# A two-layer streaming encoder on one core: plain first pairs and combinations made behind them

## Chip, cores and metric

The kernel runs on one core of a Trainium2 chip. The metric is the time of one execution in microseconds (us); lower is better. PE is TensorE, DVE is VectorE, ACT is ScalarE, POOL is GpSimd, SP is SyncE, whose queue issues the weight loads.

## What is computed

Two layers work on 656 tokens (16 meta and 512 prompt tokens, 8 x 16 sample tokens) of width 1024:

```
def swiglu(x, w_gate, w_up, w_down):
    return (jax.nn.silu(x @ w_gate) * (x @ w_up)) @ w_down
h = x + 0.5 * swiglu(rmsnorm(x, n1), f1g, f1u, f1d)
u = rmsnorm(h, nm)
...                         # pooling, gated convolution and attention on u @ w_in, gated and summed
h = h + mixed @ w_out
out = h + 0.5 * swiglu(rmsnorm(h, n2), f2g, f2u, f2d)
```

The feed-forward width is 2816, that is 22 column blocks of 128. The change is in the four feed-forward stages (two in each layer); the mixer between them stays.

## The kernel before, in words

Activations lie transposed: H holds 8 row blocks (m) of 128 features by 656 tokens. Every fp32 operand is split into a high and a low fp32r part, and a product is three matmuls (`mm3`, line 140). A split (`split`, line 145) is a copy on ACT and a subtraction on DVE (line 129).

**Strassen pairs.** Two weight columns make a pair. Four row blocks against four others, and the first half of the tokens against the second, give x as four blocks B11, B12, B21, B22 for each row pair (k, k+4). `combine` (line 529) multiplies them by the norm's gain and the old scale, makes four differences (Q1, T3, Q2, T4) and splits the seven that are used into XR, 2296 columns at once. `run_pair` (line 628) then makes seven products instead of eight, each of 4 k x 3 = 12 matmuls of 128x328 (`seven`, line 674), into three PSUM banks: the bank "mm" takes products 1, 4, 6 and 7 one on top of the other and is copied out by ACT after the first three of them, two banks "z" take the others. The seventh is put behind the first product of the unit that follows (`late`). A stage has 11 pairs, each a gate unit and an up unit; in the last stage the halves have 320 columns.

**Weights.** SP loads 512 KB blocks into four raw buffers; each unit splits seven slabs of 128x512 from them into a ring of nine slots (`ffn_columns`, line 250; one of them lies in XR). Four sums of weights for each unit are made on POOL (`sums`, line 386, recorded as line 389).

**Entry of a stage.** While the last 8 down or w_out units finish the row blocks of H in the order 0, 4, 1, 5, 2, 6, 3, 7, `feed` (line 503) squares each on ACT, adds the squares on POOL (line 518) and calls `combine` for a row pair when its second block is done. At the end the sum is split, `scales` (line 557) multiplies it by a matrix of 1/1024 in two fp32r matmuls, and the factor is made for the evictions. In the first stage `begin` (line 1137) transposes the tokens, makes the scale of both halves and then combines the four row pairs.

**Order.** What one engine does is in order. The order of each engine's instructions is fixed when the program is built: a scheduler runs the program against estimated durations and takes the ready instruction that stands first in the program. `pump` (line 357) is where the program asks for loads and slab splits.

Of the kernel before, what the change touches and what calls it, by code (L numbers as in the profile page):

```python
# [5 lines left out]
F32 = mybir.dt.float32  # L6
F32R = mybir.dt.float32r
# [39 lines left out]
XC = 2 * 4 * 7 * 328  # L47
# [4 lines left out]
WARM = 9  # L52


class Builder:
    def __init__(self, nc, tc, pools, t):
        self.nc, self.tc, self.t = nc, tc, t
        self.sb, self.wp, self.rp, self.pp = pools
        self.halves = HALF_ALL
        self.jobs = []  # L60
        self.job = self.before = None
        self.mid, self.end = [], []
        self.clock = 1
        self.held = [False, False]
        self.taken = False
        self.bank_i = 0
        self.uid = 0
# [5 lines left out]
        self.fed = 0  # L73


        self.spots = {"slab": [None] * 4, "raw": [None] * 2}
        self.spot_i = {"slab": 0, "raw": 0}
        self.busy = {"slab": [], "raw": []}
# [72 lines left out]
    def setup(self):  # L151
# [6 lines left out]
        self.ones = sb.tile([P, P], F32R, tag="ones", name="ones")  # L158
# [13 lines left out]
        self.sqs = [self.XR[:, XC + 656 * i:XC + 656 * (i + 1)] for i in range(2)]  # L172
# [27 lines left out]
        self.copies = [W[:, o + 1312 * i:o + 1312 * (i + 1)] for i in range(2)]  # L200
        self.parts = W[:, o:o + 2624]
        self.sq_row = W[:, o:o + DM]
        self.ms = W[:, o + 1024:o + 1030]
        self.rows = [W[:, o + 2000:o + 2128], W[:, o + 2128:o + 2256]]
# [4 lines left out]
        self.na_f, self.nb_f = W[:, o + 1968:o + 2296], W[:, o + 2296:o + 2624]  # L209
        o += 2624  # L210
        self.s3 = [W[:, o + 512 * i:o + 512 * (i + 1)] for i in range(2)]
        o += 1024
        assert o <= WA
# [289 lines left out]
    def feed(self, to, l, m, hi):  # L503

        c0, c1 = self.halves[hi]
        gain = {"mixer": "mix_norm", "ffn1": "ffn1_norm", "ffn2": "ffn2_norm"}[to]
        if to == "mixer":
            self.gained(self.H[:, m, c0:c1], l, m, c0, c1, gain)
        if hi == 0:
            return  # L510
        c0 = self.halves[0][0]
        n = c1 - c0
        acc, s = self.acc[:, :n], self.sq[self.fed % 2][:, :n]
        if self.fed == 0:
            self.act(acc, self.H[:, m, c0:c1], AF.Square)
        else:
            self.act(s, self.H[:, m, c0:c1], AF.Square)
            self.nc.gpsimd.tensor_tensor(acc, acc, s, op=ALU.add)  # L518
        self.fed += 1
        if to != "mixer" and m >= 4:  # L520
            self.combine(l, m - 4, gain)
# [7 lines left out]
    def combine(self, l, j, gain):  # L529


        c0, c1 = self.halves[0][0], self.halves[1][1]
        n = (c1 - c0) // 2
        p = self.parts[:, :8 * n].rearrange("p (q c) -> p q c", q=8)
        two = lambda a: a.rearrange("p (t c) -> p t c", t=2)
        scale = two(self.rstd[:, c0:c1])
        for m, out in ((j, p[:, 0:8:7, :]), (j + 4, p[:, 1:3, :])):
            self.stt(out, two(self.H[:, m, c0:c1]), self.col(gain, l, m), scale, ALU.mult, ALU.mult)
        b11, b21, b22, q1, t3, q2, t4, b12 = (p[:, i, :] for i in range(8))
        self.sub(p[:, 3:5, :], p[:, 0:3:2, :], b12.unsqueeze(1).broadcast_to([P, 2, n]))  # L540
        self.stt(q2, q1, -1.0, b22, ALU.mult, ALU.subtract)
        self.stt(t4, q2, -1.0, b21, ALU.mult, ALU.subtract)
        hi, lo = (self.XR[:, self.xc(s, j, 0, n):self.xc(s, j, 7, n)] for s in range(2))
        self.split(hi, lo, self.parts[:, :7 * n])

    @staticmethod
    def xc(s, k, q, n):
        return (s * 4 + k) * 7 * 328 + q * n
# [56 lines left out]

    def ffn_ready(self):
        self.ffn_raw()
        self.Ra = self.sb.tile([P, 2, 6, T], F32R, tag="Ra", name=self.name("ra"))

    def ffn_units(self, l, which, to):  # L610
        t = self.t
        g, up, dn = (t[f"ffn{which}_w_{s}"] for s in ("gate", "up", "down"))
        units, down = [], []
        for ci, (f0, fn) in enumerate(CHUNKS):
            for i in range(fn):
                f = 2 * (f0 + i)
                units.append(self.pair_unit(g[l], f, self.gate_out))
# [4 lines left out]
            for m in (0, 4, 1, 5, 2, 6, 3, 7):  # L622
                down.append(self.unit(k, [(0, k, dn[l][r0:r0 + k * P, m * P:(m + 1) * P])], self.hu_down, "F",
                                      m=m, l=l, scale=0.5, to=to if ci == len(CHUNKS) - 1 else None,
                                      last=ci == len(CHUNKS) - 1))
        return units + down

    def run_pair(self, u):
# [4 lines left out]
        p1, u2, u3, p5 = (self.copies[u["turn"]][:, i * n:(i + 1) * n] for i in range(4))  # L633
# [5 lines left out]
        self.seven(u, b1, 0, n, True)  # L639
        self.act(p1, b1[:, :n], AF.Copy)  # L640
# [4 lines left out]
        self.seven(u, b3, 1, n, True)  # L645
        self.tt(s[0], b3[:, :n], p1, ALU.add)
        self.pump(1)
        self.seven(u, b2, 3, n, True)
        self.act(p5, b2[:, :n], AF.Copy)
        self.pump(1)  # L650
        self.seven(u, b1, 5, n, False)
        self.act(u2, b1[:, :n], AF.Copy)
        self.pump(1)
        self.seven(u, b2, 2, n, False)
        self.tt(s[1], b2[:, :n], u2, ALU.add)
# [3 lines left out]
        self.seven(u, b1, 4, n, False)  # L659
        self.act(u3, b1[:, :n], AF.Copy)  # L660
        self.tt(s[3], u3, p5, ALU.add)
# [3 lines left out]
        def last():  # L665
            self.late = None
            self.seven(u, b1, 6, n, False)
# [6 lines left out]
    def seven(self, u, bank, q, n, start):  # L674
# [3 lines left out]
        for k in range(4):  # L678
            x = [self.XR[:, self.xc(s, k, q, n):self.xc(s, k, q + 1, n)] for s in range(2)]
# [395 lines left out]
    def mixer_units(self, l):  # L1075
# [32 lines left out]
        for m in (0, 4, 1, 5, 2, 6, 3, 7):  # L1108
# [28 lines left out]
    def begin(self):  # L1137

        nc, xt = self.nc, self.xt
        nc.vector.memset(self.factor, 1.0)  # L1140
        for hi in range(2):
            c0, c1 = HALF_ALL[hi]
            n = c1 - c0
            sums = self.psum("aux")
            for i, o, rows in self.TOKENS[hi]:
                ms = self.ms[:rows, i:i + 1]
                self.act(self.sq_row[:rows, :], xt[:rows, i, :], AF.Square, scale=DM ** -0.5, accum_out=ms)
            for m in range(KD):
                ps = self.psum(("z", "z", "z", "z", "mm", "mm", "z", "z")[m])
                for i, o, rows in self.TOKENS[hi]:  # L1150
                    nc.tensor.transpose(ps[:, o:o + rows], xt[:rows, i, m * P:(m + 1) * P],
                                        self.ident[:rows, :rows])
                nc.vector.tensor_copy(self.H[:, m, c0:c1], ps[:, :n])
            for i, o, rows in self.TOKENS[hi]:
                self.mm(sums[:, o:o + rows], self.ms[:rows, i:i + 1].broadcast_to([rows, P]), self.ident[:rows, :rows],
                        o == 0, False)
            self.scale_of(sums[:, :n], c0, c1, False, self.sil, self.up)
        for j in range(4):
            self.combine(0, j, "ffn1_norm")
            self.pump()  # L1160
        self.Ra = self.sb.tile([P, 2, 6, T], F32R, tag="Ra", name=self.name("ra"))
# [328 lines left out]
```

## Time and profile before

| | |
|---|---|
| median of 3 runs | 2926.77 us (2923.93 to 2928.16) |
| profiled execution, its time / its span | 2924.71 us / 2923.0 us |
| PE, DVE, ACT, POOL busy | 97%, 69%, 45%, 22% of the span |
| granted TensorE clock, mean | 0.982 of full speed |
| PE matmuls | 19083 |

Busy shares are averages over stages with different limits. Matmuls are pipelined, so a busy PE is not PE at its peak; the number of matmuls in a stretch of known length says more. A clock of 1.00 is the 2.4 GHz level, 0.5 the 1.2 GHz level. Lines are often those of a helper (129 is any two-input DVE operation, 126 any with a scalar, 115 any activation, 138 any matmul), so tiles tell the operations apart: XR holds the blocks and combinations of x, "ws" and "slabs" are weight slabs, "mm", "z" and "aux" are PSUM banks, "Wa" is scratch space.

### The profile page before, as it was taken

Reading aid. Unit: us, or ns where it says so; the run is one execution under the profiler, and the core shown is the slowest. Engines: PE = TensorE matmul, PEld = TensorE weight load, DVE = VectorE, ACT = ScalarE, POOL = GpSimd, SP = SyncE. Lnnn points to the kernel's source line nnn. Section 1 sums busy time; section 2 is a strip of 40 time slices with the busy share of each in tenths; the row PEclk is TensorE's granted clock in tenths of the full one; section 3 lists DMA queues with packets and bytes.
Section 4 is the critical chain, followed back from the end, with each engine's and each line's share of the span. In section 5 each row is a group of like instructions: output and inputs, shape, how many; then the busy total and the mean of one; then the engine's idle time right before and its main releaser. Section 6 shows DMA issues by size and latency. Waiting matters only on the chain.

```text
span 2923.0 us, 47652 instructions
## 1 busy us (share of the span) xinstructions
PE 2831.0 (97%) x19083; PEld 2781.1 (95%) x19083; DVE 2003.9 (69%) x3234; ACT 1322.4 (45%) x2545; POOL 652.8 (22%) x518
## 2 busy tenths in 40 slices
PE   4999999999999989999989999999999998999999
PEld 3999999999999989999979999998999998999999
DVE  7775766776444787675887866758764457975864
ACT  3443534667422354443444534446763333543533
POOL 2332232011000152232243232310110003432230
PEclk6999999999999999999989999999999999999999
DMA  2322322222222223322212222222222222322322
GB/s 83 92 64 84 87 77 70 80 73 75 62 77 73 73 69 91 87 69 84 80 48 83 83 77 87 73 75 71 76 75 66 73 76 83 87 69 83 87 76 69
DMA packets 437169, 224.26 MB, mean 77 GB/s; under 512 B 10111, under 2 KB 436291, under 8 KB 436947
## 3 DMA queue, kind: packets, MB, share of 16 engines
q1 hardware_dynamic: 436452, 220.90, 26.0%
q8 instruction: 149, 2.44, 0.3%
q14 instruction: 74, 0.60, 0.1%
q10 hardware_dynamic: 494, 0.32, 0.0%
HBM read 212.87 MB, written 8.31 MB: 76 GB/s over the span
## 4 chain that ended last, share of the span: by engine, by line
PE 85%; DVE 10%; issue 2%; ACT 2%; DMA 1%; POOL 1%; SPq 0%; ACTq 0%; DVEq 0%; POOLq 0%
PE z L138 50%; PE mm L138 33%; DVE Wa L129 2%; DVE Wa L126 2%; DVE slabs L129 2%; DVE ws L129 2%; DVE XR L129 1%; ACT XR L115 1%; PE aux L138 1%; DVE ra L129 1%; DVE H L126 0%; DMA rawb<-in_ffn_w_up_dram 0%; POOL raw L389 0%; POOL Wa L389 0%; DMA raw<-in_ffn_w_gate_dram 0%
## 5 line engine op out<-in xcount | busy, mean ns | idle before, releaser
L138 PE MATMUL mm<-XR,ws 128*128 128x328 f32 (+3 forms) x4788 | 800.7, 316 | 43.4 <-ACT XR L115 30.5
L138 PEld LDWEIGHTS mm<-XR,ws 128*128 128x128 f32 x4788 | 734.5, 189 | 53.4 <-ACT XR L115 32.0
L138 PE MATMUL z<-XR,ws 128*128 128x328 f32 (+3 forms) x3480 | 559.0, 314 | 7.1 <-DVE ws L129 7.1
L138 PEld LDWEIGHTS z<-XR,ws 128*128 128x128 f32 x3480 | 532.0, 190 | 8.6 <-DVE ws L129 8.5
L129 DVE TENSOR_TENSOR ws<-raw,ws 128x512 fp32r<-128x512 f32 (+1 forms) x413 | 312.3, 759 | 167.2 <-ACT ws L115 166.0
L115 ACT ACTIVATE ws<-raw 128x512 fp32r<-128x512 f32 (+1 forms) x413 | 253.7, 616 | 315.0 <-PE z L138 177.0
L138 PE MATMUL z<-ra,ws 128*128 128x328 f32 (+1 forms) x2520 | 395.6, 312 | 0.0
L138 PEld LDWEIGHTS z<-ra,ws 128*128 128x128 f32 x2520 | 379.9, 188 | 0.4 <-DVE H L126 0.3
L138 PE MATMUL mm<-XR,slabs 128*128 128x328 f32 (+1 forms) x1932 | 323.2, 314 | 11.3 <-ACT XR L115 5.5
L138 PEld LDWEIGHTS mm<-XR,slabs 128*128 128x128 f32 x1932 | 298.0, 189 | 15.1 <-DVE Wa L126 6.6
L138 PE MATMUL z<-ra,slabs 128*128 128x328 f32 (+1 forms) x1836 | 288.3, 312 | 0.4 <-DVE ra L129 0.4
L138 PEld LDWEIGHTS z<-ra,slabs 128*128 128x128 f32 x1836 | 277.6, 188 | 1.1 <-DVE ra L129 1.0
L129 DVE TENSOR_TENSOR Wa<-Wa 128x656 f32<-128x656 f32 (+5 forms) x328 | 253.3, 782 | 18.3 <-ACT Wa L115 14.2
L126 DVE SCALAR_TENSOR_TENSOR H<-z,H 128x328 f32<-128x328 f32 (+1 forms) x288 | 140.8, 492 | 140.3 <-PE z L138 139.9
L138 PE MATMUL z<-XR,slabs 128*128 128x328 f32 (+1 forms) x1356 | 224.9, 314 | 4.0 <-DVE H L126 2.9
L138 PEld LDWEIGHTS z<-XR,slabs 128*128 128x128 f32 x1356 | 209.3, 190 | 4.9 <-DVE H L126 3.5
L518 POOL TENSOR_TENSOR Wa<-Wa 128x656 f32<-128x656 f32 (+1 forms) x35 | 64.9, 1854 | 630.7 <-ACT Wa L115 626.8
L115 ACT ACTIVATE Wa<-Wa 128x656 f32<-128x656 f32 (+8 forms) x232 | 137.4, 598 | 120.3 <-DVE Wa L129 99.0
L129 DVE TENSOR_TENSOR slabs<-rawb,slabs 128x512 fp32r<-128x512 f32 (+1 forms) x167 | 143.6, 861 | 46.3 <-ACT slabs L115 34.3
L115 ACT ACTIVATE slabs<-raw 128x512 fp32r<-128x512 f32 (+1 forms) x163 | 98.2, 604 | 163.3 <-PE z L138 84.5
L115 ACT ACTIVATE slabs<-rawb 128x512 fp32r<-128x512 f32 (+1 forms) x167 | 100.2, 601 | 152.1 <-PE z L138 81.2
L389 POOL TENSOR_TENSOR rawb<-rawb 128x512 f32<-128x512 f32 x97 | 144.1, 1488 | 101.2 <-DVE ws L129 53.8
(179 smaller groups left out, 3508.2 us busy)
## 6 DMA issues: line engine op xcount, KB each, us to landing
raw<-in_w_in_dram SPq DMA_DIRECT2D x88, 512.0 KB, 3.7
raw<-in_ffn_w_gate_dram SPq DMA_DIRECT2D x57, 512.0 KB, 3.6
rawb<-in_ffn_w_up_dram SPq DMA_DIRECT2D x55, 512.0 KB, 3.6
rawb<-in_ffn_w_down_dram SPq DMA_DIRECT2D x48, 384.0 KB, 3.5
raw<-in_ffn_w_down_dram SPq DMA_DIRECT2D x48, 384.0 KB, 3.5
raw<-in_ffn_w_up_dram SPq DMA_DIRECT2D x33, 512.0 KB, 3.6
rawb<-in_ffn_w_gate_dram SPq DMA_DIRECT2D x31, 512.0 KB, 3.7
raw<-in_w_out_dram SPq DMA_DIRECT2D x16, 512.0 KB, 4.0
```

Of the source, the lines that this page charges most:

```text
L115: i = self.nc.scalar.activation(out, in_, func, **kw).ins
L126: return self.nc.vector.scalar_tensor_tensor(out, in0, scalar, in1, op0=op0, op1=op1).ins
L129: self.nc.vector.tensor_tensor(out, in0, in1, op=op)
L138: self.nc.tensor.matmul(out, lhsT, rhs, start=start, stop=stop, skip_group_check=True)
L389: add = lambda out, a, b: self.nc.gpsimd.tensor_tensor(out, a, b, op=ALU.add)
L518: self.nc.gpsimd.tensor_tensor(acc, acc, s, op=ALU.add)
```

## The change

- The first pair of each stage is plain: four units of one column (`col_unit`), 2 slabs each, 8 k x 3 matmuls for each token half, no weight sums; the rest stay Strassen pairs.
- x lies in XR as four blocks and four combinations. Blocks are split when their row of H arrives; combinations of the first two row pairs are made during the last units of the stage before, those of the other two behind the plain products (`todo`).
- In the first stage the first token half is prepared and split before the second, and the four plain columns take the first half, then the second (`by_half`).
- The sum of squares is not split any more: `ones` is fp32 and one fp32 matmul takes the sum. The last square is added on DVE.
- In a Strassen unit the third product of the bank "mm" is no longer copied by ACT; DVE adds from the bank.
- The slab ring in a feed-forward stage has eight slots, because XR is full.

```diff
-        at = [W[:, i * SLAB:(i + 1) * SLAB] for i in range(4)] + [self.XR[:, XC + 1312:XC + 1312 + SLAB]]
+        at = [W[:, i * SLAB:(i + 1) * SLAB] for i in range(4)]
...
+        if to != "mixer":
+            self.blocks(l, m, gain, c0, n // 2)
...
+            if self.fed == KD - 1:
+                self.tt(acc, acc, s, ALU.add)
+            else:
+                self.nc.gpsimd.tensor_tensor(acc, acc, s, op=ALU.add)
...
-            sq = [a[:, :n] for a in self.sqs]
-            self.split(sq[0], sq[1], acc)
...
+    def blocks(self, l, m, gain, c0, n):
+        j, r = m % 4, m // 4
+        p = self.part(j)[:, 2 * n * r:2 * n * (r + 1)]
+        self.stt(p, self.H[:, m, c0:c0 + 2 * n], self.col(gain, l, m), self.rstd[:, c0:c0 + 2 * n], ALU.mult, ALU.mult)
+        self.split(*(self.xs(s, j, 2 * r, n, 2) for s in range(2)), p)
+        if r:
+            self.todo.append(lambda: self.combine(j, n))
+            if j in (1, 2):
+                self.todo.pop(0)()
+    def combine(self, j, n):
+        p = self.part(j)[:, :4 * n]
+        self.mix(*(p[:, i * n:(i + 1) * n] for i in range(4)))
+        self.split(*(self.xs(s, j, Q2, n, 4) for s in range(2)), p)
+    def mix(self, b11, b12, b21, b22):
+        self.sub(b22, b22, b12)
+        self.sub(b12, b11, b12)
+        self.stt(b11, b11, -1.0, b22, ALU.mult, ALU.subtract)
+        self.stt(b21, b11, -1.0, b21, ALU.mult, ALU.subtract)
...
-            for i in (1, 0):
-                self.mm(ps, self.ones, self.sqs[i][:, c0 - at:c1 - at], i == 1, i == 0)
+            self.mm(ps, self.ones, self.acc[:, c0 - at:c1 - at], True, True)
...
+    def run_col(self, u):
+        slabs = self.use(u, 2)
+        u["w"] = [(ws, k) for ws, _ in slabs for k in range(4)]
+        cols = [(u, 0), (u, 1)]
+        if self.by_half:
+            self.held_cols.append((u, slabs))
+            cols = [(u, 0)]
+            if "last_col" in u:
+                cols += [(v, 1) for v, _ in self.held_cols]
+        for v, hi in cols:
+            self.slot_start()
+            self.half_col(v, hi)
+            if self.by_half and hi:
+                self.used(self.held_cols.pop(0)[1])
+            if self.todo and not (self.by_half and hi == 0 and v is self.held_cols[0][0]):
+                self.todo.pop(0)()
+            self.pump()
+            self.slot_tail()
...
+    def half_col(self, u, hi):
+        (c0, c1), r = self.halves[hi], u["r"]
+        n = c1 - c0
+        x = lambda s, k, a, b: self.xs(s, k % 4, 2 * (k // 4) + hi, n)
+        ps = self.product(self.psum("z"), u["w"], x, SLOTS, SLOTS, c0, c1)
+        S = self.sil if u["evict"] == self.gate_out else self.up
+        self.mul(S[:, (2 * r + hi) * n:(2 * r + hi + 1) * n], ps, self.factor[:, c0:c1])
+        if hi:
+            u["evict"](u, r, n)
...
-        self.act(u3, b1[:, :n], AF.Copy)
-        self.tt(s[3], u3, p5, ALU.add)
+        self.tt(s[3], b1[:, :n], p5, ALU.add)
...
+        sums = [self.tokens(0)]
+        self.token_scale(0, sums[0])
+        self.pump(2)
+        first = [self.parts[:, 328 * m:328 * (m + 1)] for m in range(KD)]
+        self.first_blocks(0, first)
+        sums.append(self.tokens(1))
+        self.token_scale(1, sums[1])
+        self.pump(2)
+        more = self.sb.tile([P, KD * 328], F32, tag="Ra", name="xpart")
+        second = [more[:, 328 * m:328 * (m + 1)] for m in range(KD)]
+        self.first_blocks(1, second)
+        for j in range(4):
+            self.todo.append(lambda j=j: self.first_combine(j, first, second))
```

## Rows read from the trace of the kernel before

**Rows 1.** The page: PE's busy time, the granted clock in 40 slices, the last chain.
```profile
PE 2831.0 (97%) x19083; PEld 2781.1 (95%) x19083; DVE 2003.9 (69%) x3234; ACT 1322.4 (45%) x2545; POOL 652.8 (22%) x518
...
PEclk6999999999999999999989999999999999999999
...
PE 85%; DVE 10%; issue 2%; ACT 2%; DMA 1%; POOL 1%; SPq 0%; ACTq 0%; DVEq 0%; POOLq 0%
```

**Rows 2.** Stretches: length, PE, PEld, DVE, ACT, POOL busy (instructions), clock, DMA, GB/s.
```profile
41.00:75.00 34.00, 20.59 (x73) 17.96 (x74) 24.50 (x25) 9.54 (x10) 0.00 (x0) 0.61 0.02 5
75.00:100.00 25.00, 25.00 (x168) 25.00 (x167) 19.77 (x28) 13.23 (x25) 10.44 (x7) 1.00 0.30 89
100.00:150.00 50.00, 49.98 (x333) 49.71 (x332) 37.68 (x57) 20.98 (x39) 13.86 (x10) 1.00 0.31 90
1031.00:1055.00 24.00, 16.03 (x79) 15.09 (x78) 22.91 (x22) 9.61 (x17) 18.18 (x10) 0.72 0.30 88
1055.00:1100.00 45.00, 43.72 (x288) 43.10 (x288) 40.69 (x62) 26.19 (x50) 16.50 (x10) 1.00 0.24 71
1484.00:1520.00 36.00, 22.04 (x92) 19.31 (x91) 32.15 (x40) 16.68 (x25) 13.92 (x7) 0.67 0.10 29
2471.00:2495.00 24.00, 14.89 (x88) 14.10 (x87) 22.96 (x23) 11.13 (x19) 17.50 (x10) 0.86 0.30 88
2495.00:2530.00 35.00, 32.17 (x217) 31.39 (x216) 33.90 (x48) 19.07 (x36) 14.94 (x9) 1.00 0.26 76
```

**Rows 3.** Waits of PE, whole run: us in total, times, longest.
```profile
PE mm L138 <- ACT XR L115: 36.1, 5, 21.9
PE aux L138 <- DVE XR L129: 11.8, 3, 6.2
PE mm L138 <- DVE Wa L126: 8.5, 13, 1.5
```

**Rows 4.** Timeline of DVE at the second stage's entry: start us, us, instruction.
```profile
1036.97 0.48 DVE L126 SCALAR_TENSOR_TENSOR H<-z,H 128x328 f32<-128x328 f32 x1
1037.38 0.68 DVE L129 TENSOR_TENSOR slabs<-raw,slabs 128x512 fp32r<-128x512 f32 x1
...
1038.85 2.00 DVE L129 TENSOR_TENSOR slabs<-raw,slabs 128x512 fp32r<-128x512 f32 x1
...
1047.50 2.57 DVE L129 TENSOR_TENSOR XR<-Wa,XR 128x2296 fp32r<-128x2296 f32 x1 [0.98 <-ACT XR L115]
```

**Rows 5.** The start: DVE's slab splits from 15 to 30 us; timeline to 50 us.
```profile
15.00:30.00 15.00, 10.29 (x8) 0.66 0.25 69
...
29.72 0.54 DVE L126 SCALAR_TENSOR_TENSOR scale<-Wa 128x384 f32<-128x384 f32 x1
...
40.98 0.64 PE L138 MATMUL mm<-XR,ws 128*128 128x328 f32 x1 [21.93 <-ACT XR L115]
...
43.55 1.84 DVE L126 SCALAR_TENSOR_TENSOR Wa<-H,cols,scale 128x656 f32<-128x656 f32 x2
...
45.42 0.84 DVE L129 TENSOR_TENSOR Wa<-Wa 128x656 f32<-128x656 f32 x1
...
49.52 2.55 DVE L129 TENSOR_TENSOR XR<-Wa,XR 128x2296 fp32r<-128x2296 f32 x1 [2.18 <-ACT XR L115]
```

**Rows 6.** Groups by form: line engine op tiles form xcount | busy, mean ns | idle before.
```profile
L389 POOL TENSOR_TENSOR rawb<-rawb 128x512 f32<-128x512 f32 x97 | 144.1, 1488 | 101.2 <-DVE ws L129 53.8 <-DVE slabs L129 34.4 <-DVE XR L129 9.9
L129 DVE TENSOR_TENSOR slabs<-rawb,slabs 128x512 fp32r<-128x512 f32 x145 | 133.7, 922 | 35.4 <-ACT slabs L115 34.3
L129 DVE TENSOR_TENSOR Wa<-z,Wa 128x328 f32<-128x328 f32 x148 | 72.7, 491 | 46.5 <-PE z L138 41.2 <-ACT ws L115 5.1
L138 PE MATMUL aux<-XR,ones 128*128 128x328 f32 x16 | 3.9, 370 | 5.6 <-DVE XR L129 5.6
L138 PE MATMUL aux<-Wb,poolw 128*128 128x384 f32 x8 | 3.2, 484 | 0.0
```

**Rows 7.** Waits of PE from 75 to 480 us, the first stage after its entry.
```profile
PE mm L138 <- DVE Wa L126: 2.5, 4, 0.8
```

More of the change, by code (lines that the diff above doesn't have):

```diff
@@ L43 @@
 CW = CP + NB * CS
-XC = 2 * 4 * 7 * 328
 XR = 20992
@@ L52 @@
 WARM = 9
+B11, B12, B21, B22, Q2, Q1, T4, T3 = range(8)
+SLOTS = (0, 4, 1, 5, 2, 6, 3, 7)
 class Builder:
@@ L199, in setup @@
         o += 656
-        self.copies = [W[:, o + 1312 * i:o + 1312 * (i + 1)] for i in range(2)]
+        self.copies = [W[:, o + 328 * i:o + 328 * (i + 1)] for i in range(2)]
         self.parts = W[:, o:o + 2624]
-        self.sq_row = W[:, o:o + DM]
-        self.ms = W[:, o + 1024:o + 1030]
-        self.rows = [W[:, o + 2000:o + 2128], W[:, o + 2128:o + 2256]]
         o += 2624
@@ L526, in feed @@
             halves = self.halves
             self.pending = lambda: self.scales(to, halves)
[L529 to L544, printed above, removed]
@@ L604, in pair_unit, with col_unit @@
                     run=self.run_pair, evict=run, ring="F", turn=int(self.turn), **kw)
+    def col_unit(self, w, f, r, run):
+        return dict(slabs=[4, 4], src=[(KD, [(0, KD, w[:, (f + r) * P:(f + r + 1) * P])])], prep=self.prep_plain,
+                    run=self.run_col, evict=run, ring="F", r=r, i=0)
+    def run_col(self, u):
[16 more added lines that the diff above has]
+            self.slot_tail()
+        if not self.by_half:
+            self.used(slabs)
+        elif "last_col" in u:
+            self.by_half = False
+    def half_col(self, u, hi):
[7 more added lines that the diff above has]
+            u["evict"](u, r, n)
     def ffn_ready(self):
@@ L616, in ffn_units @@
                 f = 2 * (f0 + i)
+                if ci == i == 0:
+                    for w, out in ((g[l], self.gate_out), (up[l], self.up_out)):
+                        units += [self.col_unit(w, f, r, out) for r in range(2)]
+                    units[-1]["last_col"] = True
+                    continue
                 units.append(self.pair_unit(g[l], f, self.gate_out))
@@ L632, in run_pair @@
         b1, b2, b3 = self.psum("mm"), self.psum("z"), self.psum("z")
-        p1, u2, u3, p5 = (self.copies[u["turn"]][:, i * n:(i + 1) * n] for i in range(4))
+        p5 = self.copies[u["turn"]][:, :n]
         f = self.factor[:, c0:c0 + 2 * n]
@@ L678, in seven @@
         for k in range(4):
-            x = [self.XR[:, self.xc(s, k, q, n):self.xc(s, k, q + 1, n)] for s in range(2)]
+            x = [self.xs(s, k, q, n) for s in range(2)]
             self.mm3(bank[:, :n], ws[:, 0, k, :], ws[:, 1, k, :], x[0], x[1], start and k == 0, k == 3)
@@ L1158, in begin @@
[L1158 to L1161, printed above, removed]
+        self.nc.vector.memset(self.factor, 1.0)
+        sums = [self.tokens(0)]
[5 more added lines that the diff above has]
+        self.token_scale(1, sums[1])
@@ new lines, in token_scale, with first_blocks, first_combine @@
+    def token_scale(self, hi, sums):
+        c0, c1 = HALF_ALL[hi]
+        self.scale_of(sums, c0, c1, False, self.sil, self.up)
+    def first_blocks(self, hi, parts):
+        n = 328
+        c = slice(n * hi, n * (hi + 1))
+        for m in SLOTS:
+            j, r = m % 4, m // 4
+            self.stt(parts[m], self.H[:, m, c], self.col("ffn1_norm", 0, m), self.rstd[:, c], ALU.mult, ALU.mult)
+            self.split(*(self.xs(s, j, 2 * r + hi, n) for s in range(2)), parts[m])
+    def first_combine(self, j, first, second):
+        n = 328
+        self.mix(first[j], second[j], first[j + 4], second[j + 4])
+        for hi, parts in ((0, first), (1, second)):
+            for r in range(2):
+                self.split(*(self.xs(s, j, Q2 + 2 * r + hi, n) for s in range(2)), parts[j + 4 * r])
```

83 lines of the change are left out of this document (46 added, 37 removed).

## The prediction

> **What bounds the kernel now.** I read the page first [rows 1]. TensorE is busy for 97% of the span and the chain that ended last is 85% PE, so the kernel is a stream of 128x328 matmuls, and time can come only from fewer matmuls or from the 92 us in which PE is idle or slowed. The slices of the granted clock hint at where: the first is at 6 tenths, and one in the middle at 8.
>
> Next I cut the span at the feed-forward entries [rows 2]. In an undisturbed stretch, 100 to 150 us, PE runs 333 matmuls in 50 us at clock 1.00, that is 0.150 us each (0.150 x 320/328 = 0.146 us in the last stage, where they have 320 columns). Against that rate I count what each entry loses. Start: 73 + 168 = 241 product matmuls by 100 us are worth 36.2 us, so 63.8 us are lost. Second stage, 1031 to 1100: 79 + 288 = 367 are worth 55.1 of 69 us, 13.9 lost. Third, 1484 to 1520: 92 are worth 13.8 of 36, 22.2 lost. Fourth, 2471 to 2530: 305 are worth 44.5 of 59, 14.5 lost. The granted clock is 0.61, 0.72, 0.67 and 0.86 there, so a gap costs twice: PE idles, and then runs part of the next products at its 1.2 GHz level.
>
> Then the waits of PE over the whole run [rows 3]: 36.1 us for the activation that writes combinations into XR, 11.8 us, in three waits of up to 6.2, where the matmul for the sum of squares stands in PE's queue ahead of its input, 8.5 us for a PSUM bank that VectorE (DVE) has to read. The timeline of DVE at the second entry shows what is late behind all of them [rows 4]: a weight split takes 2.00 us beside the POOL sums of the pair's weights and 0.68 us without, the last H update comes at 1037, and the last combination is split at 1047.5, all of it with DVE busy for 22.9 of 24 us [rows 2]. At the start [rows 5] the scale of the first half is written at 29.7, PE begins at 41.0, and the next combination is split 8.5 us later, at 49.5; two more follow. So DVE sets the entries.
>
> **The change part by part.**
>
> Plain first pair. A Strassen pair unit is 7 x 12 = 84 matmuls, a plain one 2 columns x 2 halves x 24 = 96. Two units in four stages: 96 matmuls more, 24 x 0.150 = 3.6 us a stage (3.5 in the last), all on PE's path. Certain cost 14.3 us. Against it: 8 slabs instead of 14 a stage, which at 0.68 us [rows 4] frees 4.1 us of DVE, and eight POOL sums of 1.49 us [rows 6] fall away, each of which can lengthen a DVE split by 2.00 - 0.68 = 1.3 us [rows 4]. I take 8 us of relief an entry; the bounds are 0, if the next pair's sums move into the same place, and 10.
>
> Blocks as H arrives, combinations behind. The last row block now needs one gain multiply (0.92 us), an activation of 656 columns and one subtraction (0.84) before PE has it; before, it was two multiplies (1.84), a difference (0.84), two smaller steps and a split of 2296 columns, 2.55 us on DVE alone [rows 5]. The first plain product takes its row blocks in the order in which they come, so all but the last two blocks of the eight can run early, in up to four PSUM banks: 4 x 18 = 72 matmuls, 10.8 us of cover. Over all of an entry DVE's work for the combinations hardly changes (per row pair 1.84 + 0.84 + 2 x 0.49 + 2.55 = 6.2 us before; 1.84 + 2 x 0.84 + 4 x 0.49 + 1.5 = 7.0 after, the 1.5 an estimate between the rows for 656 and 2296 columns), but half of it moves behind the entry, under 28.9 us of plain products. If that cover is short, the stall reappears at the first Strassen pair, which needs Q1 at its third product.
>
> Sum of squares. The split of the sum (656 columns on ACT and DVE) goes, and the last add goes from POOL to DVE. The sum's matmul becomes one full-precision matmul. The trace has none of this shape; the nearest is that of the pool map, 8 records for 4 calls of 384 columns, 3.2 us, so 0.80 us a call, 0.68 for 328; two fp32r matmuls take 0.49 [rows 6]. Ten of them: 2.0 us more (from 0, where PE is idle anyway, to 4). The Trainium skill, "FP8 and Floating Point Precision", TensorE Precision Notes, says that true FP32 is four passes; against two passes here that would double the 0.49 us, 4.9 us in all, and the sum below would be 2.9 us worse. The pool map's row is measured, so I keep 2.0.
>
> Third product straight from PSUM. 80 remaining Strassen units lose an ACT copy (the chain has 2% of ACT in it [rows 1]: worth nothing), and DVE reads the bank itself, at 0.49 us, as in its other sums from PSUM [rows 6]. But the seventh product adds into that bank, with one product of 12 x 0.150 = 1.8 us between; if DVE is later than that, PE's whole queue stands behind it. PE waited on DVE for such banks only 2.5 us, four times, in the whole first stage [rows 7]. I charge 2.5 us over all stages; the bounds are 0 and, with 0.45 us in each of the 80 units (0.92 us, the mean split of the slabs' row, and the 0.49 us sum, after 0.84 us of another step, less 1.8), 35.
>
> One slab fewer in the ring. XR holds eight blocks, so eight slabs instead of nine: look-ahead falls from 16.3 to 14.5 us of products. Outside the entries PE hardly waits for slabs [rows 7]; I charge 2 us, bounds 0 and 7.2 (one product of 1.8 us in each of four stages). The weight loads stay in their order on SP's queue, four of 512 KB at the start, and nothing is moved past another queue.
>
> Start. Eight splits stand on DVE before the first half's scale, 10.3 us in all [rows 5], lengthened by the POOL sums; without the sums 8 x 0.68 = 5.4, so the scale comes at about 24 us instead of 29.7. The first half's blocks cost 8 x (0.49 + 0.49) = 7.8 us on DVE: first block at 25, last at 32. PE starts at 25 and not at 41, with 96 matmuls (14.4 us) of the first half, plus about 3 us at the lower clock: done at 42. DVE then makes the second half's scale (1.8), four evictions (2.0) and eight blocks (7.8), by 43.6, so PE goes on nearly without a gap and ends the plain pair at about 57. Behind it come four combinations of 8 x 0.49 = 3.9 us each, four evictions, up's product and split and some eight slabs: 15.7 + 2 + 3.3 + 6.5, to 71. The Strassen pair's first two products need none of it (3.6 us), the rest waits: I take 5.5 us. Pair one is then done, in effect, at 62.5 us; before, at 63.8 + 168 x 0.150 = 89.0. Gain 26.5, between 16 (later scale, longer low clock) and 32 (no stall).
>
> Later entries, gap before less plain matmuls less what I leave as remaining stall: 13.9 - 3.6 - 3 = 7.3; 22.2 - 3.6 - 4 = 14.6; 14.5 - 3.5 - 3 = 8.0. The stalls left are my choice, about a fifth of each gap; the bounds are 0 and the whole old gap less the relief of DVE. The two entries into the mixers change little: their product order is untouched and their shorter sum is not charged or credited.
>
> Sum: 26.5 + 7.3 + 14.6 + 8.0 - 2.0 - 2.5 - 2.0 = 49.9 us. The profiled execution took 2924.7 us (1.7 around its span), so 2874.8; it lies 2.1 us under the median of 2926.8, which makes 2877.
>
> **The rivals.**
>
> The stall moves to the first Strassen pair. DVE still has all its work, and its queue is in order. For it: DVE is 89 to 96% busy in the entries (22.91 of 24, 32.15 of 36, 22.96 of 24 us) [rows 2]. Against it: fewer slabs, no POOL sums, 28.9 us of cover. Then only the relief remains, 8 us an entry in three entries less 10.7 of matmuls, and 16 at the start, less the small costs: 24 - 10.7 + 16 - 6.5 = 23, 2904 us. Chance 0.20.
>
> The gaps stay. The order on each engine is fixed ahead of the run, on estimated durations; if PE's queue holds a combination's product or the sum ahead of work that is ready, as the waits for the sum show it can [rows 3], the plain pair buys nothing in the later stages. Gain 16 at the start, less 10.7 and small costs: about 2927, no change. Chance 0.06.
>
> Slower: the seventh product waits for DVE's read of the third. Place: every remaining pair unit. Two lengthened splits ahead make 2 x 2.00 + 0.49 - 1.8 = 2.7 us a unit, 216 us in 80 units. It decides from 50 / 80 = 0.63 us a unit on. For it: DVE splits average 0.92 us in the slabs' rows, so lengthened ones are common [rows 6]. Against it: [rows 7], where the same engine releases banks with little loss. At 1 us a unit: 2877 - 2.5 + 80 = 2955. Chance 0.08.
>
> **How the numbers follow.** Forecast 0.66, moved stall 0.20, no change 0.06, slower 0.08. A measurement of this kernel can tell about 0.2%, 5.9 us, from none. The forecast's own range is 2850 to 2895 (start bounds, stalls from 0 to twice mine, ring and bank costs); the moved stall adds up to 2906. Faster 0.86, same 0.06, slower 0.08.
>
> **What would show it.** Right: PE's first product at 23 to 28 us; 0 to 4 us of PE idle at each later entry with the clock near 1.00; waits of PE for XR from ACT under 10 us in all; no wait for the sum over 2 us; 96 more product matmuls, 24 fewer splits, 32 fewer POOL sums. Wrong: PE waiting at Q1 of the second pair for 8 us or more; many waits of "mm" for a DVE sum into Wa; DVE splits at an entry still near 2 us.

## The result and the profile after

The changed kernel takes 2890.89 us (median of 4 runs, 2889.91 to 2893.26) against 2925.52 of the kernel before on the same chip: ratio 0.9882, 95% interval 0.9865 to 0.9899, so 34.6 us less (29.6 to 39.5). The profiled execution's span went from 2923.0 to 2888.3 us, 34.7 less.

The page of the changed kernel, PE's busy time and the granted clock (beside [rows 1]):

```profile
PE 2829.0 (98%) x19179; PEld 2781.5 (96%) x19179; DVE 1936.6 (67%) x3262; ACT 1289.9 (45%) x2464; POOL 598.2 (21%) x481
...
PEclk8999999999999999999999999999999999999999
```

There are the 96 more matmuls, and the clock's weak slices are gone but for the first, 8 tenths instead of 6. Line numbers of helpers have moved by five (129 is 134 now, 138 is 143).

Where the time came from is read best between fixed points of the work. The five sums of squares (matmuls on the tile "ones", one at each entry) are such points. The instructions on that tile, one stretch after the other, in the kernel before (records, ns min/median/max, first to last start):

```profile
L138 PE MATMUL aux<-XR,ones x4: 307/310/314, 514.9 to 515.3; 128*128 128x328 f32 x4
L138 PE MATMUL aux<-XR,ones x4: 475/475/639, 1045.0 to 1045.9; 128*128 128x328 f32 x4
L138 PE MATMUL aux<-XR,ones x4: 312/316/422, 1505.6 to 1506.2; 128*128 128x328 f32 x4
L138 PE MATMUL aux<-XR,ones x4: 313/314/315, 1956.9 to 1957.4; 128*128 128x328 f32 x4
L138 PE MATMUL aux<-XR,ones x4: 468/468/636, 2484.4 to 2485.4; 128*128 128x320 f32 x4
```

and in the changed kernel:

```profile
L143 PE MATMUL aux<-Wa,ones x4: 439/439/439, 487.7 to 488.6; 128*128 128x328 f32 x4
L143 PE MATMUL aux<-Wa,ones x4: 438/438/439, 1010.8 to 1011.6; 128*128 128x328 f32 x4
L143 PE MATMUL aux<-Wa,ones x4: 437/438/439, 1469.6 to 1470.4; 128*128 128x328 f32 x4
L143 PE MATMUL aux<-Wa,ones x4: 438/439/439, 1918.8 to 1919.6; 128*128 128x328 f32 x4
L143 PE MATMUL aux<-Wa,ones x4: 430/432/433, 2439.3 to 2440.1; 128*128 128x320 f32 x4
```

The differences of the starts say it: the first stage, with the start, became 27.2 us shorter (514.9 to 487.7). First mixer and second stage together went from 990.7 to 981.9 (8.8 less), the third stage from 451.3 to 449.2 (2.1 less), second mixer and last stage, up to the end of the span, from 966.1 to 969.5 (3.4 more). Mixer and stage are taken together since the old kernel's gap lay ahead of the sum and the new one's lies behind it. The third stage starts at such a gap too, so its 2.1 can't be told apart cleanly from the 8.8 before it; the total of the three can. So nearly the whole gain is the start, and everything behind it brought 7.5 us.

The same stretches as [rows 2], in the changed kernel: the start, then the three later entries.

```profile
0.00:50.00 50.00, 32.70 (x178) 26.76 (x179) 37.56 (x78) 29.30 (x62) 8.31 (x17) 0.83 0.46 142
50.00:75.00 25.00, 25.00 (x168) 24.94 (x167) 23.55 (x42) 14.82 (x30) 12.73 (x6) 1.00 0.20 56
75.00:100.00 25.00, 24.60 (x164) 24.33 (x163) 21.01 (x33) 11.64 (x22) 4.17 (x3) 1.00 0.25 72
...
1000.00:1050.00 50.00, 47.37 (x312) 46.76 (x311) 39.48 (x55) 21.27 (x34) 15.83 (x11) 1.00 0.31 90
1450.00:1500.00 50.00, 43.84 (x267) 42.95 (x266) 41.74 (x57) 20.08 (x31) 12.67 (x8) 0.93 0.15 43
2430.00:2500.00 70.00, 66.14 (x429) 65.56 (x428) 51.20 (x80) 31.84 (x54) 16.95 (x13) 0.95 0.28 82
```

At 0.150 us each (0.146 in the last stage) 333 matmuls fit into 50 us and 480 into the 70. In the last three rows 21, 66 and 51 are missing. That is 20.5 us lost, 17.3 of them at the third and fourth entry, where the granted clock falls too (0.93 and 0.95). The waits of PE over the whole run say on what it stood (us in total, times, longest; beside [rows 3]):

```profile
PE mm L143 <- DVE Wa L134: 20.3, 19, 1.8
PE z L143 <- DVE Wa L134: 10.1, 3, 3.9
PE z L143 <- ACT XR L120: 6.5, 1, 6.5
PE z L143 <- DVE XR L134: 5.8, 2, 3.3
```

The 36.1 us of waits for combinations and the 11.8 for the sum are gone. The last two rows are waits for blocks of x: 6.5 and 3.3 us at the start, 2.6 at the third entry. Two kinds of wait in the later stages are new. **The entry:** three waits of a z bank (2.6, 3.6 and 3.9 us, one at each later entry) for an eviction of the plain pair. **The pairs:** 18 waits of up to 1.6 us of the seventh product, which adds into the bank "mm", for DVE's direct read of the third product there (the nineteenth, 1.8 us, lies in a mixer). The timelines show how each comes about. First the pair at 415 us, on POOL, ACT, DVE and PE:

```profile
406.40 1.30 POOL L394 TENSOR_TENSOR Wa<-rawb 128x512 f32<-128x512 f32 x1 [8.53 <-DMA rawb<-in_ffn_w_up_dram]
...
410.83 0.63 ACT L120 ACTIVATE ws<-raw 128x512 fp32r<-128x512 f32 x1 [5.76 <-POOL raw L394]
...
411.49 1.22 DVE L134 TENSOR_TENSOR ws<-raw,ws 128x512 fp32r<-128x512 f32 x1 [3.09 <-ACT ws L120]
...
413.99 0.68 DVE L134 TENSOR_TENSOR ws<-Wa,ws 128x512 fp32r<-128x512 f32 x1
414.59 0.49 DVE L134 TENSOR_TENSOR Wa<-mm,Wa 128x328 f32<-128x328 f32 x1
...
415.13 2.08 PE L143 MATMUL mm<-XR,slabs 128*128 128x328 f32 x12 [1.55 <-DVE Wa L134]
```

A weight load lands late, and POOL's sums of weights start when it lands. ACT stands 5.76 us until a sum is made, and DVE stands 3.09 us for ACT's copy. The read of the bank is queued behind that split and three more DVE instructions, and PE's queue stands behind the read. Then the fourth entry, DVE, POOL and PE:

```profile
2447.45 1.46 DVE L131 SCALAR_TENSOR_TENSOR scale<-Wa 128x320 f32<-128x320 f32 x1
2448.64 1.42 POOL L394 TENSOR_TENSOR rawb<-rawb 128x512 f32<-128x512 f32 x1
2448.84 2.57 DVE L134 TENSOR_TENSOR XR<-Wa,XR 128x1280 fp32r<-128x1280 f32 x1
2451.33 0.48 DVE L134 TENSOR_TENSOR Wa<-scale 128x320 f32<-128x320 f32 x1
...
2453.66 10.45 PE L143 MATMUL z<-XR,slabs 128*128 128x320 f32 x51 [3.85 <-DVE Wa L134]
```

The scale is there at 2448.9, but the factor made from it (Wa<-scale) waits behind the 2.57 us split of a combination, and the first two evictions start at 2453.1, after three more DVE instructions. The z banks stay full until then. The split itself is lengthened: a POOL sum of the next pair's weights runs beside it, and eight splits of nearly the same shape (1312 columns) take 1.65 us on average.

### The profile page after: what moved, and what is told of

It reads as the page before. It is cut to its first block, busy times and chain, and to the rows that moved or that the text cites. A ratio compares the mean times of both kernels' runs of the same rounds, so it can differ in the third digit from the quotient of the medians.

```text
span 2888.3 us, 47733 instructions
## 1 busy us (share of the span) xinstructions
PE 2829.0 (98%) x19179; PEld 2781.5 (96%) x19179; DVE 1936.6 (67%) x3262; ACT 1289.9 (45%) x2464; POOL 598.2 (21%) x481
## 3 DMA queue, kind: packets, MB, share of 16 engines
q1 hardware_dynamic: 436452, 220.90, 26.2%
## 4 chain that ended last, share of the span: by engine, by line
PE 81%; DVE 10%; POOL 4%; DMA 3%; ACT 1%; issue 1%; ACTq 0%; SPq 0%; POOLq 0%; DVEq 0%
PE z L143 50%; PE mm L143 29%; DVE Wa L134 2%; DMA rawb<-in_ffn_w_up_dram 2%; DVE ws L134 2%; DVE Wa L131 2%; DVE slabs L134 2%; POOL rawb L394 1%; POOL raw L394 1%; DVE XR L134 1%; POOL Wa L394 1%; DMA raw<-in_ffn_w_gate_dram 1%; PE aux L143 1%; ACT ws L120 0%; DVE ra L134 0%
## 5 line engine op out<-in xcount | busy, mean ns | idle before, releaser
L143 PE MATMUL z<-XR,ws 128*128 128x328 f32 (+3 forms) x3924 | 629.2, 313 | 13.5 <-ACT XR L120 6.5
L143 PEld LDWEIGHTS z<-XR,ws 128*128 128x128 f32 x3924 | 597.1, 189 | 15.3 <-ACT XR L120 6.8
L143 PE MATMUL z<-ra,slabs 128*128 128x328 f32 (+1 forms) x2112 | 330.9, 312 | 1.8 <-ACT ra L120 1.8
L143 PE MATMUL z<-XR,slabs 128*128 128x328 f32 (+1 forms) x1764 | 296.6, 316 | 9.7 <-DVE Wa L134 6.5
L143 PEld LDWEIGHTS z<-XR,slabs 128*128 128x128 f32 x1764 | 275.1, 192 | 11.2 <-DVE Wa L134 7.0
L134 DVE TENSOR_TENSOR Wa<-Wa 128x656 f32<-128x656 f32 (+5 forms) x245 | 204.3, 834 | 3.9 <-ACT Wa L120 0.2
L134 DVE TENSOR_TENSOR ws<-rawb,ws 128x512 fp32r<-128x512 f32 (+1 forms) x183 | 147.9, 812 | 83.2 <-ACT ws L120 82.9
L120 ACT ACTIVATE Wa<-Wa 128x656 f32<-128x656 f32 (+7 forms) x232 | 136.9, 597 | 122.6 <-DVE Wa L134 113.6
L134 DVE TENSOR_TENSOR slabs<-raw,slabs 128x512 fp32r<-128x512 f32 (+1 forms) x183 | 145.9, 799 | 61.7 <-ACT slabs L120 61.5
L120 ACT ACTIVATE ws<-rawb 128x512 fp32r<-128x512 f32 (+1 forms) x183 | 108.3, 599 | 172.5 <-PE z L143 94.7
```

Source lines behind the costliest of these rows:

```text
L120: i = self.nc.scalar.activation(out, in_, func, **kw).ins
L134: self.nc.vector.tensor_tensor(out, in0, in1, op=op)
L143: self.nc.tensor.matmul(out, lhsT, rhs, start=start, stop=stop, skip_group_check=True)
```

## The experiments

Two theories for the gain that is missing in the pairs came first: T, that DVE's direct read of the third product costs it, and R, that the lost slab slot does. P grew out of the first results: splits that wait for late weights stand in DVE's queue ahead of that read. F is the theory for the entries: the plain pair's evictions wait for the factor. The runs, each against the kernel before on the same chip:

| kernel | median us | ratio, interval |
|---|---|---|
| changed kernel | 2890.89 | 0.9882, 0.9865 to 0.9899 |
| e_copy | 2875.99 | 0.9836, 0.9822 to 0.9849 |
| e_ring9 | 2882.14 | 0.9853, 0.9840 to 0.9867 |
| e_ring7 | 2870.03 | 0.9816, 0.9803 to 0.9829 |
| e_copy_ring7 | 2871.09 | 0.9813, 0.9800 to 0.9827 |
| b_direct (kernel before, edited) | 2935.13 | 1.0037, 1.0024 to 1.0051 |
| b_ring8 (kernel before, edited) | 2932.46 | 1.0022, 1.0013 to 1.0031 |
| e_banks | 2875.69 | 0.9831, 0.9818 to 0.9844 |
| e_nofactor | 2875.49 | 0.9827, 0.9814 to 0.9840 |
| e_nohalf | 2886.21 | 0.9862, 0.9849 to 0.9876 |
| e_strassen_first | 2905.06 | 0.9927, 0.9915 to 0.9940 |
| e_banks_ring7 | 2858.19 | 0.9761, 0.9747 to 0.9774 |
| e_onesum | 2850.00 | 0.9736, 0.9723 to 0.9750 |

The kernel before took 2922.2 to 2927.1 us on the chips of these runs, so differences between two rows of medians can be off by some 3 us. They are given below by medians, with those by the ratios where the argument hangs on the size.

**The third product's read, and the ring.** (In e_ring9 the slot is added at a stage's first Strassen pair and taken away ahead of the last down units; its diff is cut to the first.)

```diff
 e_copy
-        self.tt(s[3], b1[:, :n], p5, ALU.add)
+        self.act(s[3], b1[:, :n], AF.Copy)
+        self.tt(s[3], s[3], p5, ALU.add)
 b_direct
-        self.act(u3, b1[:, :n], AF.Copy)
-        self.tt(s[3], u3, p5, ALU.add)
+        self.tt(s[3], b1[:, :n], p5, ALU.add)
 e_ring7, in run_pair
+        del self.spots["slab"][7:]
 e_ring9, spare and its call in run_pair
+    def spare(self, n):
+        x = self.XR.rearrange("p (s k c) -> p s k c", s=2, k=4)
+        return [x[:, :, :, B12 * n + i * P:B12 * n + (i + 1) * P] for i in range(1)]
...
+        if len(self.spots["slab"]) == 8 and not self.slabs[self.n_prep][0].get("last"):
+            self.spots["slab"] += self.spare(n)
```

> The changed kernel with the ACT copy of the third product of bank mm put back (copied into the place of the result, then added on DVE). The changed kernel has 20.3 us of PE waits for an mm bank that DVE has to read into Wa. Theory T (the direct read is what cost about 14 us more than forecast): these waits fall under 8 us and the time falls by 8 to 18 us from 2890.9, to about 2879. Rival R (the lost slab slot: weights come late, and whatever stands in DVE's queue behind a late split is late with it): the bank is freed by ACT, whose queue has the same late splits, so the time changes by less than 4 us.

> The kernel before with one part of the change alone: DVE adds the third product of bank mm straight from PSUM, no ACT copy. Nine slots as before. Theory T: 8 to 15 us slower than before, 2934 to 2940, with mm waits for DVE in Wa up from 11 to about 20 us. Rival R: within 3 us of before (2925.5), as the prediction's 2.5 us for this part.

> The changed kernel with a ninth slab slot: block B12 is used by the plain pair alone, so after it its columns in XR hold a slab, until the slabs of the last down units are made. Theory R: weights come one product (1.8 us) earlier again, the late splits go, 8 to 15 us less than 2890.9, about 2880, and the mm waits fall with them. Rival T: the waits for DVE's read stay near 20 us, and the time changes by less than 3 us.

> The changed kernel with one slab slot less (seven) in the Strassen pairs of each stage. Theory R: a slot is worth 10 us or more at this depth, so over 2901. Rival T: a slot is worth 2 us, as the prediction charged, so 2891 to 2895.

T held when the read was taken out and when it was put in alone. With the copy back the time falls by 14.9 us (13.5 by the ratios). Of 20.5 us of waits for a bank "mm" to be read 12.2 are left, 5.5 of them for ACT:

```profile
PE mm L143 <- ACT Wa L120: 5.5, 8, 1.4
PE mm L143 <- DVE Wa L131: 4.9, 5, 1.4
...
PE mm L143 <- DVE Wa L134: 1.8, 1, 1.8
```

Not all of the gain is the read's: the three entries' stretches hold 17 more matmuls than the changed kernel's, 2.5 us, though the edit doesn't act there.

Put into the kernel before alone, the direct read costs 13.0 us by the medians on this chip, 10.8 by the ratio (interval 7 to 15), and in it the waits rise from 8.5 and 2.5 us to:

```profile
PE mm L138 <- DVE Wa L126: 12.8, 11, 3.1
...
PE mm L138 <- DVE Wa L129: 5.9, 7, 1.7
```

R fell with seven slots and held with nine, and T missed both. Seven slots, which should have been slower by R and no faster by T, are 20.9 us faster than eight (19.3 by the ratios). Nine are 8.8 us faster (8.5 by the ratios, with intervals that just overlap). PE's waits for the direct read fall with them, as R had it, while other waits for that bank come up:

```profile
PE mm L143 <- DVE Wa L131: 8.3, 4, 2.5
...
PE mm L143 <- DVE Wa L134: 2.2, 2, 1.8
```

So one slot fewer and one more both help, and a slot has no price of its own. What seven slots change is seen in ACT's groups of weight copies (busy, mean ns | idle before, releasers), the changed kernel first:

```profile
L120 ACT ACTIVATE slabs<-raw 128x512 fp32r<-128x512 f32 x159 | 99.2, 628 | 200.3 <-PE z L143 79.9 <-POOL raw L394 57.7 <-PE mm L143 46.6
L120 ACT ACTIVATE ws<-rawb 128x512 fp32r<-128x512 f32 x159 | 98.7, 627 | 162.6 <-PE z L143 91.0 <-POOL rawb L394 39.7 <-PE mm L143 24.4
```

and with seven slots:

```profile
L120 ACT ACTIVATE ws<-rawb 128x512 fp32r<-128x512 f32 x177 | 110.4, 628 | 129.6 <-PE z L143 84.0 <-PE mm L143 34.4 <-POOL rawb L394 5.6
L120 ACT ACTIVATE slabs<-raw 128x512 fp32r<-128x512 f32 x141 | 87.7, 627 | 125.7 <-PE z L143 61.4 <-POOL raw L394 18.4 <-PE mm L143 18.1
```

Over the four groups of copies from raw buffers, the idle time that a POOL sum ended falls from 27.0 + 57.7 + 39.7 + 29.4 = 153.8 us to 11.2 + 5.6 + 18.4 + 19.2 = 54.4, and the mm waits for DVE from 20.3 to 4.2 us. P explains both: with less room splits are queued later, when their sum is made already, and the read behind them isn't held up. The rows fit this, but no run shows the order of the queue as the cause by itself. For nine slots P doesn't fit: ACT waits 44.5 + 20.8 + 45.8 + 28.6 = 139.7 us for sums there, nearly as long as in the changed kernel, and yet the read's waits are gone. R's account, weights that are split earlier, would do for nine but not for seven; why both are faster stays open.

> The kernel before with one part of the change alone: eight slab slots instead of nine. Seven slots made the changed kernel 21 us faster and nine made it 9 us faster, so look-ahead as such isn't what a slot is worth. Theory P (what counts is which splits stand, waiting for late weights, ahead of an urgent read of PSUM in DVE's queue; the number of slots only changes that order, and before, ACT freed the third product's bank): within 5 us of before. Theory R8 (eight slots against units of seven slabs are bad in themselves): 8 to 20 us slower than before.

> The changed kernel with both edits: ACT copies the third product of bank mm, and seven slots in the Strassen pairs. Alone the edits gave 15 and 21 us. Theory P (both take away the same waits of the seventh product): 2866 to 2873, about as with seven slots alone. Rival (two separate costs, the read and the ring): they add up, 2853 to 2860.

The two edits don't add up: 2871.1, the time of seven slots alone. So seven slots and the copy take away the same cost, as P has it. Eight slots in the kernel before cost 6.4 us by the ratio (interval 3.8 to 9.1), a little over P's bound and under R8's: which of the two it is isn't settled.

```diff
 e_onesum
             add(s3, a11, a21)
-            add(a21, a21, a22)
-            add(a11, a21, a11)
-            add(a12, a11, a12)
```

> The changed kernel without three of the four POOL sums of each Strassen unit (those that are made in the raw buffers), so that four of seven products use unsummed weights; the copies, splits and matmuls stay as many. Theory P (splits of late sums stand ahead of the read of the third product in DVE's queue): the mm waits for DVE fall from 20.3 us to under 8, and the time by 12 to 20 us, 2871 to 2879. Rival (the weight loads themselves are late, or DVE simply has too much queued there): the waits stay over 14 us and the time within 5 us of 2890.9.

All 18 waits in the pairs go, only the mixer's is left:

```profile
PE mm L143 <- DVE Wa L134: 1.8, 1, 1.8
...
PE z L143 <- DVE Wa L134: 0.9, 1, 0.9
```

That is P's sign, but the gain is 40.9 us and not 12 to 20, because the entry's waits go too (10.1 us before, 0.9 now). DVE's busy time falls from 1936.6 to 1837.6 us with the same 3262 instructions. So this run shows the sums as the source of both waits, but not by lateness alone: sums that run beside DVE lengthen its steps. At the fourth entry of this run the step that writes the scale takes 0.49 us and the combination's split 1.48, against 1.46 and 2.57 in the changed kernel (above), and PE waits 0.9 us there instead of 3.9. The Trainium skill, "Trainium Architecture — The Big Picture", What this means for kernel authors, says that VectorE and GpSimd contend for a shared port pair, by an exclusive lock. These 99 us agree with the contention; whether it is a lock they don't show. Seven slots show that shorter steps aren't needed for the gain in the pairs: the four groups of splits take 746 to 896 ns there on average, in the changed kernel 747 to 863.

**The factor at the entries.**

```diff
 e_banks, in half_col
-        ps = self.product(self.psum("z"), u["w"], x, SLOTS, SLOTS, c0, c1)
+        tag = ("z", "z", "z", "z", "mm", "mm", "z", "z")[self.col_i % 8]
+        self.col_i += 1
+        ps = self.product(self.psum(tag), u["w"], x, SLOTS, SLOTS, c0, c1)
 e_nofactor, in half_col
-        self.mul(S[:, (2 * r + hi) * n:(2 * r + hi + 1) * n], ps, self.factor[:, c0:c1])
+        self.mul(S[:, (2 * r + hi) * n:(2 * r + hi + 1) * n], ps, self.H[:, 0, c0:c1])
```

> The changed kernel, with the fifth and sixth half column of each stage's plain pair in the two mm banks, which are free there: six half columns (21.6 us) instead of four (14.4 us) fit ahead of the first eviction, which needs the factor. Theory F (the factor is the last wait of the later entries: 2.6, 3.6 and 3.9 us of PE waits, with the clock at 0.93 to 0.95 behind two of them): those three waits go, 10 to 16 us less than 2890.9. Rival (DVE as a whole sets the entry; another of its operations is late next): the waits move to the blocks or to Q1 of the second pair, less than 4 us gained.

> The changed kernel with the factor left out of the evictions of the plain pair: they multiply by a row block of H, which is there long before, so the result is another one; work and banks stay the same. Theory F: the three waits of 2.6, 3.6 and 3.9 us go, as with more banks, 10 to 16 us less than 2890.9. Rival: less than 4 us, and if this is much more than with the banks, it is not the number of banks that limits.

F held, twice with the same size: 15.2 and 15.4 us. Two more banks do all that the missing factor does. The entries' stretches with the banks:

```profile
1000.00:1050.00 50.00, 50.00 (x331) 49.66 (x330) 44.73 (x60) 23.85 (x38) 16.76 (x11) 1.00 0.32 95
1450.00:1500.00 50.00, 47.33 (x310) 46.45 (x309) 46.43 (x62) 22.81 (x37) 19.24 (x12) 1.00 0.20 58
2430.00:2500.00 70.00, 70.00 (x475) 69.68 (x475) 58.04 (x89) 34.66 (x59) 20.99 (x15) 1.00 0.34 100
```

19 + 43 + 46 = 108 more matmuls than in the changed kernel are 16 us, the whole gain, and the clock is 1.00. The 2.6 us of waits for blocks at the third entry stay (2.2 us in this run).

**The plain pair and the token halves.**

```diff
 e_strassen_first
-            self.todo.append(lambda: self.combine(j, n))
-            if j in (1, 2):
-                self.todo.pop(0)()
+            self.combine(j, n)
...
-                if ci == i == 0:
+                if ci == i == 0 and (l, which) == (0, 1):
...
-        self.act(s[0], b1[:, :n], AF.Copy)
+        p1 = self.parts[:, 2296:2296 + n] if self.pending else s[0]
+        self.act(p1, b1[:, :n], AF.Copy)
...
-        self.tt(s[0], b3[:, :n], s[0], ALU.add)
+        self.tt(s[0], b3[:, :n], p1, ALU.add)
 e_nohalf
-        self.by_half = True
+        self.by_half = False
```

> The changed kernel with the plain first pair in the first stage alone: in the three later stages the first pair is a Strassen pair again, all combinations are made as the rows of H arrive, and the first product is copied out into a free part of the scratch space while the sum of squares still needs the usual one. Blocks are still split apart from combinations. Theory (the plain pair is the cover): the gaps of before come back, 50.6 us in three entries, less 10.7 of matmuls saved and the 15 that the changed kernel still loses there: 18 to 30 us slower than 2890.9, 2909 to 2921. Rival (splitting row by row is what helps; the plain pair buys little): within 5 us of 2890.9.

> The changed kernel without the token halves in turn in the first stage: each of the four plain columns takes both halves, as in the later stages. In the changed kernel PE runs the first half of all four columns from 28.3 to about 48 us, and the blocks of the second half are made beside it. Theory: now the second half column has to wait for the second half's blocks, which are done at about 44 us, and 7 to 12 us are lost, 2898 to 2903. Rival (DVE's total of work sets the start; the combinations for the second pair come no later): less than 3 us.

The plain pair is the cover, but it is worth less than expected: 14.2 us (13.2 by the ratios), not 18 to 30. The entries without it:

```profile
1000.00:1050.00 50.00, 41.19 (x245) 38.61 (x244) 45.61 (x58) 23.67 (x40) 19.06 (x13) 0.93 0.21 64
1450.00:1500.00 50.00, 38.52 (x201) 35.46 (x200) 47.16 (x62) 23.45 (x37) 24.50 (x12) 0.83 0.15 43
2430.00:2500.00 70.00, 59.74 (x379) 56.92 (x378) 65.58 (x82) 33.80 (x56) 29.71 (x19) 0.98 0.26 75
```

67 + 66 + 50 = 183 fewer matmuls than in the changed kernel are 27.2 us. But 72 fewer have to be run (10.7 us), so 16.5 us should be lost, near the 14.2 measured. Against the full rate these stretches lose 47.7 us, where the three gaps of before were 50.6. So the gaps come back almost whole, and splitting row by row without the plain pair wins some 3 us at most. The forecast was too high because it took 15 us for what the changed kernel still loses at its entries; with the 20.5 of its stretches it would have been 19.

The token halves brought nothing in the end; without them the kernel was 4.7 us faster, by the ratios 2.0 thousandths with intervals that overlap. The loss of 7 to 12 us that was expected didn't come. At the start there is a smaller one. PE with the halves in turn (first product, first Strassen product):

```profile
28.27 0.92 PE L143 MATMUL z<-XR,ws 128*128 128x328 f32 x2 [6.48 <-ACT XR L120]
...
62.80 1.96 PE L143 MATMUL mm<-XR,ws 128*128 128x328 f32 x12
```

and without:

```profile
30.81 0.64 PE L143 MATMUL z<-XR,ws 128*128 128x328 f32 x1 [7.51 <-ACT XR L120]
...
66.49 1.96 PE L143 MATMUL mm<-XR,ws 128*128 128x328 f32 x12
```

3.7 us are lost there, but 2.5 of them lie ahead of the first product; from it to the first Strassen product the halves in turn save 1.2 us. The last stage, which the edit doesn't touch, gives more back, 4.2 us: behind its entry PE waits 2.78 us instead of 3.85, and the clock doesn't fall (last section). Such a shift of some 5 us elsewhere comes with an edit that only re-orders the start, and is the caution for every difference of this size here; that of nine slots is not much larger.

**Both costs at once.** e_banks_ring7 has the edits of e_banks and e_ring7.

> The changed kernel with two edits: mm banks for the fifth and sixth half column of the plain pair, and seven slots in the Strassen pairs. Alone they gave 15 and 21 us. If the factor's wait at the entries and the seventh product's wait in the pairs are separate costs, they add up: 2851 to 2859. Rival (seven slots helped the entries too): 2862 to 2870.

The two costs are separate: 2858.2, 32.7 us less, of 36.1 for the two alone. The 3.4 us between are about what e_ring7 by itself had gained in the entries' stretches (20 more matmuls, 3.0 us). It beats both kernels, 2.4% under the kernel before.

## Why the prediction was right, and where its sum was not

The range, the sign and the likeliest case held (2890.9 within its own 2850 to 2895); of 49.9 us forecast 34.6 came.

- **Start: right in the sum, partly by luck.** With the first pair done at 62.8 us (forecast 62.5), 89.0 - 62.8 = 26.2 us came and 26.5 were forecast. But two misses cancel in it. PE's first product came at 28.3 us instead of 25, just past the sign's 23 to 28, and PE then waited 3.3 us for blocks, which wasn't forecast: the plain pair ended at 62.8 and not at 57. The stall of 5.5 us behind it never came; no wait of that Strassen pair is over 0.4 us. DVE had the last combination split at 64.8 us, where the forecast had its work behind the plain pair last to 71. Which part of the change carries the start no run takes apart, but for the halves in turn, which give little.
- **Entries: the step that failed.** "The stalls left are my choice, about a fifth of each gap", 10 us. The stretches above lose 20.5, and e_banks brings 15 back. The forecast credited four banks with 10.8 us of cover against late blocks and never costed what empties them: an eviction needs the factor, which is made from the last row block through ACT and DVE, and DVE makes the combinations in the same time, with POOL's sums beside it. The waits for XR in the later entries are 2.6 us at most, so the blocks were costed well; the next wait behind them was missed. The signs missed with it: at the third entry PE is idle for 6.2 us, not 0 to 4, and the clock is 0.93 and 0.95 at the last two. It isn't the rival of the moved stall, since Q1 is not waited for.
- **Third product from PSUM: mis-sized.** 2.5 us charged, 10.8 measured alone in the kernel before and 14.9 in the changed one (13.5 by the ratios). The evidence in [rows 7] held for a kernel in which ACT freed that bank. The slower rival names the right wait, but at 18.5 us in 80 units, 0.23 a unit, it stays under the 0.63 at which it decides.
- **Ring: wrong mechanism.** 2 us were charged for look-ahead. Eight slots cost 6.4 in the kernel before, but in the changed one seven and nine are both faster than eight. So look-ahead isn't what the count acts through; the order of splits is the likelier cause, not a shown one.
- **Sum of squares: right.** No wait for the entries' sums over 2 us. Four records take about 1.2 us at an entry (1010.8 to 1011.6 and the last one's 0.44) instead of 0.7 in the old first row, 0.26 us a call, 2.6 for ten; 2.0 were charged. The Trainium skill's page "FP8 and Floating Point Precision", TensorE Precision Notes, states four passes for true FP32; set against two, as the prediction does, that would double the time. The measured ratio is 1.7, under that.
- **Relief of DVE: at its lower bound.** The 24 splits and 32 POOL sums fewer came. But the next pair's sums moved into the same place, which the prediction had as the case of no relief: beside them a split at the fourth entry took 1.77 us, as one of the wrong signs had it, and the combination's split 2.57. The row that the price rested on was misread, too. Beside the split of 2.00 us in [rows 4] POOL was adding squares (line 518), not weights, and the change keeps all but the last of these adds at each entry:

```profile
1038.38 1.93 POOL L518 TENSOR_TENSOR Wa<-Wa 128x656 f32<-128x656 f32 x1 [1.88 <-ACT Wa L115]
```

Put together from the measured terms, 26.2 + (50.6 - 10.7 - 20.5) - 2.6 - 14.9 = 28.1, with the ring left in the read's term since the two don't add. That is 6.5 us short of 34.6. Of the 14.9, 2.5 lie at the entries and not in the read, and the rest is within the shifts by order seen above; what they are stays open.

## What to carry to other kernels

When a gap is filled with early work, follow that work to its end: it fills PSUM, and what empties PSUM (here a factor that the old gap hid) is the next wait. Before a copy that frees a PSUM bank is taken out, look at what stands ahead of its replacement in that engine's queue: a split that waits for a late weight holds up every urgent read behind it. And try the ring of split weights at more than one depth: a slot also changes the order in each engine's queue, and here one fewer and one more were both faster.

## What the hardware showed beyond that

After some of the entries' waits the granted clock falls, and the length of the wait doesn't tell after which. The same 51 matmuls run behind the wait for the first eviction in each of these runs. Three of them, of the runs without the token halves, e_copy and e_ring7 in turn:

```profile
2451.67 7.75 PE L143 MATMUL z<-XR,slabs 128*128 128x320 f32 x51 [2.78 <-DVE Wa L134]
...
1478.23 7.92 PE L143 MATMUL z<-XR,ws 128*128 128x328 f32 x51 [3.61 <-DVE Wa L134]
...
1019.10 9.46 PE L143 MATMUL z<-XR,slabs 128*128 128x328 f32 x51 [2.34 <-DVE Wa L134]
```

The granted clock over these matmuls, and over others of the kind:

| run, entry | wait us | 51 matmuls us | granted clock |
|---|---|---|---|
| changed kernel, second | 2.63 | 7.92 | 1.00 |
| changed kernel, third | 3.59 | 9.47 | 0.82 |
| changed kernel, fourth | 3.85 | 10.45 | 0.71 |
| e_nohalf, fourth | 2.78 | 7.75 | 1.00 |
| e_copy, third | 3.61 | 7.92 | 1.00 |
| e_copy, fourth | 2.84 | 9.28 | 0.82 |
| e_ring7, second | 2.34 | 9.46 | 0.82 |

At 1.00, the 2.4 GHz level, they take 7.75 us (320 columns) or 7.92 (328); where part of them runs at the lower level, 1.5 to 2.7 us more. A wait of 2.34 us was followed by a fall and one of 3.61 wasn't, so what else decides it these runs don't show. It makes part of the shifts by order: of the 4.2 us that e_nohalf wins in the last stage, 1.1 are a shorter wait and 2.7 the clock.
